# Low parts of some weights by a negative on ScalarE and an accumulating transfer, in place of differences on GpSimd

## The chip, the cores and the metric

The kernel runs on one core of one Trainium2 chip. The metric is the device time of one execution in microseconds (us). The engines are named as the profile names them: PE is TensorE (matmuls; PEld its weight loads), DVE is VectorE, ACT is ScalarE, POOL is GpSimd, SP is SyncE, which here only starts transfers. Each engine works through its own instructions in order.

## The reference

Two layers of an encoder over 512 positions of width 1024, in float32. Cut to what matters here:

```python
mem_n = rms_norm(mem, mem_norm_g)                  # 256 memory tokens
for l in range(2):
    h = rms_norm(x, g_pre_mix[l])
    proj = h @ w_in[l]                             # 1024 x 5632: three attentions' q, k, v, and gates
    ...                                            # neighbourhood (with bias rpb), dilated, memory (mem_n @ w_kv[l])
    x = x + rms_norm(merged @ w_out[l], g_post_mix[l])
    h = rms_norm(x, g_pre_ffn[l])
    u = depthwise_conv_centred(h @ w_up[l], conv_w[l], conv_b[l])
    x = x + rms_norm((gelu(a) * b) @ w_down[l], g_post_ffn[l])
```

## The kernel before

Activations lie transposed in SBUF: channels in the 128 partitions, positions in the free dimension, split into two halves of 256 positions. Every float32 product is made of three products of a shorter format (float32r): each operand is split into a high part (`hi`, rounded) and a low part (`lo`, the value minus `hi`), and `mm3` issues hi·hi, hi·lo and lo·hi into one PSUM bank. So each weight tile of 128x1024 is loaded raw (`wraw`, three buffers, by SP), then cast to `hi` by ScalarE, then `lo` is made by a difference raw - hi, usually on VectorE. This is `split`, called by `weights`. A buffer of `wraw` is free for the next load when its last reader is done.

Most weights are prepared as one tile of 128x1024 (`whi`, `wlo`, two buffers each) while TensorE works on the one before. At two places TensorE would have nothing to do while a norm is computed, and several weight tiles are prepared ahead as two chunks of 128x512 each, into buffers named `m` (or `h`):

- At the start of layer 0: six tiles of `w_in`, those in `FIRST`, called tile one to six below. TensorE multiplies them as three pairs with the first half of the positions as soon as that half is normalised (banks mm, mm, then o, pt, then s, s), then all with the second half. The pair five and six is the group s<-h,m.
- At the handover from layer 0 to layer 1, around the last norm of layer 0: four tiles of `w_kv` (`kv_ahead`) and the same six tiles of `w_in` for layer 1. The tables `KVE` and `GEN` say by letter which engine makes the low part: G for GpSimd, V for VectorE.

The norm needs squares of x (ScalarE), their sum over tiles (`acc`, VectorE), a matmul against a column of 1/1024 (`pt<-mean,acc`, on TensorE in its place in the order), a square root and a reciprocal. At the handover each of the eight tiles of x is first updated (y<-y,pt, then x<-x,y on VectorE).

TensorE's order is fixed by hand (`Woven`: a clock of estimated costs, jobs with due times, explicit order edges). The other engines' order comes from a scheduler that sees the dependences. GpSimd also makes the bias of the neighbourhood attention for each head (`a_bias`: a transfer of `rpb`, then three differences against a mask), copies keys (`ka`, `m`) and adds the gated branches. The bias transfer is held behind GpSimd's last difference of weights, where there is one:

```python
behind(nc.gpsimd.dma_start(out=raw, in_=rpb[l, h]).ins, last_lo.get(G))
```

Lines of the profile that matter: 114 is the line through which every ScalarE and VectorE instruction is issued, 225 a difference of `split`, 230 the raw load, 247 a matmul, 293 and 294 key copies, 455 the memory tokens' transfer (started by ScalarE), 596 and 599 the bias transfer and its differences.

Of the kernel before, what the change touches and what calls it, by code (L numbers as in the profile page):

```python
# [9 lines left out]
AF = mybir.ActivationFunctionType  # L10
ALU = mybir.AluOpType
# [9 lines left out]
KD = D_MODEL // 128  # L21
# [6 lines left out]
FIRST = (0, 3, 4, 7, 6, 1)  # L28
# [6 lines left out]

LAT_QK, LAT_SM, LAT_T, LAT_V, LAT_T2 = 1.0, 4.5, 1.5, 2.0, 0.6
STEP_A, STEP_B, STEP_M = 9.0, 9.0, 5.5
SQG, LOG, GEN, KVE = {0: (), 1: ()}, {0: (), 1: ()}, 'GGVGVG', 'VVGG'
SD1 = 4.0
MARGIN = 0.3  # L40
SB = True
# [1 line left out]
KVD, GWD, NG, LAT1 = 7.3, 1.0, 2, 12.0  # L43
# [76 lines left out]
def tile_hybrid_encoder(ctx, tc, xT, memT, memg, vecs, rpb, w_in, w_kv, w_bra, w_brb, w_brm,  # L120
                        w_out, w_up, w_down, c_ident, c_mask, c_tab0, c_tab1, out):
    nc = tc.nc
# [13 lines left out]
    uid, last_copy, last_act, crit, last_lo = [0], [None], [None], [None], {}  # L136
    wv = Woven(tc)

    def nm(s):
        uid[0] += 1  # L140
        return f"{s}_{uid[0]}"


    def big(dt=F32R, shape=(128, 512)):
        return mp.tile(list(shape), dt, tag="m", name=nm("m"))
# [28 lines left out]
    def f32(ap):  # L174
        return ap.bitcast(F32)

    G = nc.gpsimd
    ACT, V = Counted(nc.scalar, wv, 0.1, 0.8e-3), Counted(nc.vector, wv, 0.065, 1.05e-3)

    DUP, MDUP = G, G  # L180
    MSQ = G

    def ready(least):
# [34 lines left out]
    def behind(ins, other):  # L218

        if other is not None and ins is not other:  # L220
            tc.add_manual_dep(ins, other.name, ORDER, reason="issue order")

    def split(src, hi, lo, eng=None):
        last_copy[0] = ACT.copy(hi, src).ins
        last_lo[eng or V] = (eng or V).tensor_sub(lo, src, f32(hi)).ins

    def weights(src, K, C, slot=None, eng=None, after=None):

        raw = wp.tile([128, K, C], F32, tag="wraw", name=nm("wraw"))
        nc.sync.dma_start(out=raw, in_=src)  # L230
        if slot is None:
            hi = wp.tile([128, K, C], F32R, tag="whi", name=nm("whi"), bufs=2)
            lo = wp.tile([128, K, C], F32R, tag="wlo", name=nm("wlo"), bufs=2)
            split(raw, hi, lo, eng)
            behind(last_copy[0], after)
            return [(hi[:, k, :], lo[:, k, :]) for k in range(K)]
        n = 512 // C
        w = []
        for k in range(0, K, n):
            c = min(n, K - k)  # L240
            hi, lo = slot(F32R, (128, c, C)), slot(F32R, (128, c, C))
            split(raw[:, k:k + c, :], hi, lo, eng)
            w += [(hi[:, i, :], lo[:, i, :]) for i in range(c)]
        return w

# [68 lines left out]
    def sumsq_add(acc, src, first, slot=None, eng=None):  # L314
        if first:
            ACT.activation(acc, src, AF.Square)
        else:
            n = acc.shape[-1]
            sq = slot((128, 256)) if slot else small("sq2", 4) if n == 256 else small("sq", 1, (128, 512))
            ACT.activation(sq, src, AF.Square)  # L320
            (eng or V).tensor_add(acc, acc, sq)
# [34 lines left out]
    def rtile():  # L356
        return tp.tile([128, 512], F32, tag="R", name=nm("R"), bufs=1)
# [6 lines left out]
    def pre_norm_job(l, goff, acc, hs, i):  # L364
        half, box = HALVES[i], []
        yield from rstd_job(acc if isinstance(acc, list) else [acc[:, half]], 256, box)
        for k in range(KD):
            g = g0[:, k:k + 1] if l == 0 and goff == V_PRE else vec[:, l, goff + k:goff + k + 1]
            normed(xh(k, half), g, box[0], hs[k][0][:, half], hs[k][1][:, half],
                   G if k in LOG[l > 0 and goff == V_PRE] else V)  # L370
        crit[0] = last_copy[0]
        yield 1.2
        wv.give(f"h{l}.{goff}.{i}")
# [73 lines left out]
    def h_tiles():  # L447
        return [(htile(), htile()) for _ in range(KD)]


    def mem_norm_job(l, hm, slot):
        raws = []
        for k2 in range(KD // 2):
            t = slot(F32, (128, 2, N_MEM))
            nc.scalar.dma_start(out=t, in_=memT[:, 2 * k2:2 * k2 + 2, :])
            raws += [t[:, 0, :], t[:, 1, :]]
        acc = small("h32", 3)
        for k in range(KD):
            sumsq_add(acc, raws[k], k == 0, None, MSQ if l else V)
        yield 14.0  # L460
        box = []
        yield from rstd_job([acc], N_MEM, box)
        for k in range(KD):
            t = slot(F32R, (128, 2, N_MEM))
            normed(raws[k], mg[:, k:k + 1], box[0], t[:, 0, :], t[:, 1, :])
            hm.append((t[:, 0, :], t[:, 1, :]))
        yield 1.2
        wv.give(f"mem{l}")
# [10 lines left out]
    def mem_kv(l, hm, km, vm, pre=()):  # L479
        wv.need(f"mem{l}")  # L480
        for m in range(4):
            w = pre[m] if pre else weights(w_kv[l, m], KD, 128)
            ps = mmbank((128, N_MEM))
            linear(ps, w, hm, slice(0, N_MEM))
            if m < 2:
                t, u = big(F32R, (128, 2, N_MEM)), big(F32R, (128, 2, N_MEM))
                twice_split(ps, (t[:, 0, :], t[:, 1, :]), (u[:, 0, :], u[:, 1, :]), None, MDUP)
                km.append((t, u))
            else:
                vT = big(F32, (128, 256))  # L490
                ACT.copy(vT, ps)
                wv.spawn(mem_v_job(l, vT, vm))


    def group_weights(srcs, engs):
        return [weights(s, KD, 128, big, e) for s, e in zip(srcs, engs)]
# [19 lines left out]
    def proj(l, m, hs, after=None):  # L516
        w = weights(w_in[l, m], KD, 128, after=after)
        ps = mmbank()
        linear(ps, w, hs)
        return ps  # L520
# [366 lines left out]
    gw = group_weights([w_in[0, m] for m in FIRST[:2]], (V, V))  # L887
# [4 lines left out]
    with tc.issue_after(last_copy[0]):  # L892
        sqs = first_squares(HALVES[1])
    wv.spawn(pre_norm_job(0, V_PRE, sqs, hs, 1), SD1)
    gw += group_weights([w_in[0, m] for m in FIRST[2:]], (V, G, V, G))
    for t, c in ((mask, c_mask), (tab0, c_tab0), (tab1, c_tab1)):
        nc.sync.dma_start(out=t, in_=c)
    hm = []
# [3 lines left out]
    for l in range(depth):  # L902
# [41 lines left out]
        for m in range(KD):  # L944
# [3 lines left out]
            hi, lo = big(), big()  # L948
# [4 lines left out]
        hs, R, gw = h_tiles(), rtile(), []  # L953
# [44 lines left out]
        if l == depth - 1:  # L998
            sublayer_end(l, V_POSTF, w_of, fs, 2, None)
            while wv.jobs:  # L1000
                wv._step()
        else:
            hm, km, vm = [], [], []
            wv.spawn(mem_norm_job(l + 1, hm, htile), 20.0)
            pre, R, raw, box = [], rtile(), [], []

            def then(a, i, l=l, box=box):
                box.extend(h_tiles())
                return pre_norm_job(l + 1, V_PRE, a, box, i)

            gw = []

            def kv_ahead(l=l, pre=pre, gw=gw):
                pre.append(weights(w_kv[l + 1, 0], KD, 128, htile))
                yield KVD
                for i in (1, 2, 3):
                    yield 0.9
                    pre.append(weights(w_kv[l + 1, i], KD, 128, big, G if KVE[i] == 'G' else V))
                wv.give(f"kv{l + 1}")
                for m in range(NG):  # L1020
                    yield GWD
                    gw.extend(group_weights([w_in[l + 1, FIRST[m]]], [G if GEN[m] == 'G' else V]))
                wv.give(f"gw{l + 1}")

            sublayer_end(l, V_POSTF, w_of, fs, 1, [then, (box, raw, R)], (1.4, LAT1), lambda: wv.spawn(kv_ahead()))
            wv.need(f"kv{l + 1}")
            mem_kv(l + 1, hm, km, vm, pre)
            wv.need(f"gw{l + 1}")
            gw += group_weights([w_in[l + 1, m] for m in FIRST[NG:]], [G if e == 'G' else V for e in GEN[NG:]])
            wv.need(f"h{l + 1}.{V_PRE}.0")  # L1030
            hs = box

# [92 lines left out]
```

## Time and profile before

| | |
|---|---|
| median of 3 runs | 1551.14 us (1551.08 to 1551.52) |
| the profiled execution's own time | 1551.73 us |
| its span, first to last instruction | 1550.0 us |
| mean granted clock of TensorE | 0.995 |
| differences of weights on GpSimd | 16, 22.7 us in all |
| bias transfers from GpSimd's queue | 12, of 128 KB |

A row of the timeline gives start, duration (us), engine, line, operation, output<-inputs, shapes and count, and in brackets the idle time before it with what ended it. A row of the waits gives the sum in us, the number of waits and the longest. A row of the stretches gives the stretch, then busy us of PE, PEld, DVE, ACT and POOL (with the instructions that started in it), the granted clock, the share of the 16 DMA engines, and GB/s. A row of a group gives line, engine, operation and count, then busy us, mean ns, and the idle time before it by releaser. A row of a transfer gives its count, size, and the median us from issue to landing.

### The profile page before, as it was taken

Reading aid. Unit: us, or ns where it says so; the run is one execution under the profiler, and the core shown is the slowest. Engines: PE = TensorE matmul, PEld = TensorE weight load, DVE = VectorE, ACT = ScalarE, POOL = GpSimd, SP = SyncE. Lnnn points to the kernel's source line nnn. Section 1 sums busy time; section 2 is a strip of 40 time slices with the busy share of each in tenths; the row PEclk is TensorE's granted clock in tenths of the full one; section 3 lists DMA queues with packets and bytes.
Section 4 is the critical chain, followed back from the end, with each engine's and each line's share of the span. In section 5 each row is a group of like instructions: output and inputs, shape, how many; then the busy total and the mean of one; then the engine's idle time right before and its main releaser. Section 6 shows DMA issues by size and latency. Waiting matters only on the chain.

```text
span 1550.0 us, 20648 instructions
## 1 busy us (share of the span) xinstructions
PE 1522.5 (98%) x7970; PEld 1300.1 (84%) x7970; DVE 951.6 (61%) x1684; ACT 712.7 (46%) x1266; POOL 149.7 (10%) x217
## 2 busy tenths in 40 slices
PE   8999999999999999999989999999999999999997
PEld 7988888888988888888888888888889888888887
DVE  6685676335777777742497756753456977776233
ACT  5565554336544444532355555532354544444231
POOL 3340000110000000000154300002100000000000
PEclk9999999999999999999999999999999999999999
DMA  7221213235113322333431221132350233323331
GB/s 246 89 88 64 62 57 107 84 95 165 53 59 100 100 96 95 118 90 101 129 102 59 78 66 58 61 104 88 102 177 15 82 96 99 101 99 89 99 105 63
DMA packets 45810, 144.91 MB, mean 93 GB/s; under 512 B 5376, under 2 KB 9600, under 8 KB 45712
## 3 DMA queue, kind: packets, MB, share of 16 engines
q1 hardware_dynamic: 43776, 139.85, 28.5%
q10 hardware_dynamic: 1296, 2.10, 0.4%
q0 software_dynamic: 640, 1.64, 0.3%
q8 instruction: 62, 1.02, 0.3%
q14 instruction: 36, 0.29, 0.1%
HBM read 141.48 MB, written 2.10 MB: 93 GB/s over the span
## 4 chain that ended last, share of the span: by engine, by line
PE 91%; DVE 6%; ACT 2%; issue 1%; DMA 0%; SPq 0%; ACTq 0%; DVEq 0%
PE mm L247 80%; PE s L247 4%; PE o L247 3%; PE pt L258 2%; DVE m L114 1%; DVE y L114 1%; PE pt L247 1%; DVE ka L114 1%; DVE x L114 1%; ACT y L114 1%; DVE st L114 0%; DVE acc L114 0%; DMA x<-in_xT_dram 0%; DVE wlo L114 0%; ACT whi L114 0%
## 5 line engine op out<-in xcount | busy, mean ns | idle before, releaser
L247 PE MATMUL mm<-h,whi 128*128 128x512 f32 x2496 | 776.5, 392 | 0.0
L247 PEld LDWEIGHTS mm<-h,whi 128*128 128x128 f32 x2496 | 462.0, 188 | 91.3
L247 PE MATMUL mm<-h,wlo 128*128 128x512 f32 x1248 | 486.9, 390 | 0.0
L114 DVE TENSOR_TENSOR wlo<-wraw,whi 128x1024 fp32r<-128x1024 f32 (+1 forms) x213 | 259.2, 1217 | 284.7 <-ACT whi L114 282.3
L114 ACT CAST whi<-wraw 128x1024 fp32r<-128x1024 f32 (+1 forms) x213 | 221.4, 1040 | 307.8 <-PE mm L247 293.4
L247 PEld LDWEIGHTS mm<-h,wlo 128*128 128x128 f32 x1248 | 234.5, 188 | 49.6
L247 PE MATMUL mm<-m,whi 128*128 128x512 f32 (+1 forms) x800 | 215.1, 356 | 1.0 <-DVE m L114 0.8
L247 PEld LDWEIGHTS mm<-m,whi 128*128 128x128 f32 x800 | 141.8, 189 | 22.8 <-PE mm L247 1.3
L247 PE MATMUL mm<-m,wlo 128*128 128x512 f32 (+1 forms) x400 | 142.1, 355 | 0.0
L114 DVE SCALAR_TENSOR_TENSOR y<-y,vec,y 128x511 f32<-128x511 f32 x176 | 130.5, 748 | 3.5 <-ACT y L114 0.9
L114 DVE TENSOR_TENSOR y<-mm,R 128x512 f32<-128x512 f32 x82 | 56.4, 688 | 68.5 <-PE mm L247 68.5
L247 PEld LDWEIGHTS mm<-m,wlo 128*128 128x128 f32 x400 | 75.5, 189 | 10.9
L802 POOL TENSOR_TENSOR m<-m,y 128x512 f32<-128x512 f32 x28 | 36.1, 1289 | 399.4 <-DVE y L114 399.4
L114 ACT ACTIVATE y<-y,vec 128x512 f32<-128x512 f32 x88 | 71.1, 815 | 2.3 <-DVE y L114 1.9
L247 PE MATMUL mm<-m,m 128*128 128x512 f32 x240 | 63.5, 394 | 0.0
L114 ACT ACTIVATE y<-y 128x512 f32<-128x512 f32 x44 | 27.9, 633 | 71.7 <-DVE y L114 71.3
L114 ACT CAST m<-pt 128x512 fp32r<-128x512 f32 (+1 forms) x72 | 38.6, 541 | 46.8 <-PE pt L258 38.5
L114 ACT ACTIVATE y<-y,st 128x256 f32<-128x256 f32 (+1 forms) x80 | 43.8, 549 | 30.4 <-DVE st L114 28.9
L114 DVE TENSOR_TENSOR acc<-acc,sq 128x256 f32<-128x256 f32 (+1 forms) x80 | 41.1, 514 | 26.6 <-ACT sq L114 24.7
L114 DVE TENSOR_TENSOR m<-pt,m 128x512 fp32r<-128x512 f32 (+1 forms) x72 | 45.1, 630 | 19.9 <-ACT m L114 18.6
L114 ACT CAST m<-y 128x512 fp32r<-128x512 f32 x32 | 19.9, 622 | 72.5 <-DVE y L114 72.5
L247 PE MATMUL mm<-h,m 128*128 128x256 f32 x312 | 49.1, 301 | 2.0 <-ACT h L114 1.0
(154 smaller groups left out, 1789.9 us busy)
## 6 DMA issues: line engine op xcount, KB each, us to landing
wraw<-in_w_in_dram SPq DMA_DIRECT2D x88, 512.0 KB, 3.7
wraw<-in_w_up_dram SPq DMA_DIRECT2D x88, 512.0 KB, 3.6
wraw<-in_w_down_dram SPq DMA_DIRECT2D x32, 512.0 KB, 3.5
wraw<-in_w_out_dram SPq DMA_DIRECT2D x16, 512.0 KB, 3.9
wraw<-in_w_down_dram SPq DMA_DIRECT2D x16, 384.0 KB, 3.1
wraw<-in_w_kv_dram SPq DMA_DIRECT2D x8, 512.0 KB, 4.0
wraw<-in_w_bra_dram SPq DMA_DIRECT2D x16, 192.0 KB, 2.3
x<-in_xT_dram SPq DMA_DIRECT2D x8, 256.0 KB, 7.3
```

The lines of the kernel that those rows point to most:

```text
L114: return op(*args, **kw)
L247: wv.pe(nc.tensor.matmul(ps, a, b, start=first, stop=last), cost)
L258: wv.pe(nc.tensor.transpose(ps[:, 128 * i:128 * i + 128], s, ident), 0.11)
L802: (V if br == 2 and m >= 6 else G).tensor_add(acc[m], acc[m], gs)
```

## The change

A third letter, D, is added. For it ScalarE writes the high part as before, then writes the rounded negative of the raw weight into the buffer of the low part, and a transfer started from GpSimd's queue adds the raw weight from DRAM onto it. So there is no difference on any engine, but the raw weight is read from DRAM a second time (256 KB for a chunk), and the raw buffer's last reader is ScalarE. The tables replace every G: at the start the tiles three to six were V, G, V, G and are V, V, D, D; of `w_kv` the last two were G and are D; of `w_in` for layer 1 the six were G, G, V, G, V, G and are D, D, V, V, D, D.

```diff
-SQG, LOG, GEN, KVE = {0: (), 1: ()}, {0: (), 1: ()}, 'GGVGVG', 'VVGG'
+SQG, LOG, GEN, KVE = {0: (), 1: ()}, {0: (), 1: ()}, 'DDVVDD', 'VVDD'
...
+    ENG = {'G': G, 'V': V, 'D': 'D'}
...
-            split(raw[:, k:k + c, :], hi, lo, eng)
+            if eng == "D":
+                last_copy[0] = ACT.copy(hi, raw[:, k:k + c, :]).ins
+                ACT.activation(lo, raw[:, k:k + c, :], AF.Copy, scale=-1.0)
+                nc.gpsimd.dma_start(out=lo, in_=src[:, k:k + c, :], accum_op=ALU.add)
+            else:
+                split(raw[:, k:k + c, :], hi, lo, eng)
...
-    gw += group_weights([w_in[0, m] for m in FIRST[2:]], (V, G, V, G))
+    gw += group_weights([w_in[0, m] for m in FIRST[2:]], (V, V, 'D', 'D'))
...
-                    pre.append(weights(w_kv[l + 1, i], KD, 128, big, G if KVE[i] == 'G' else V))
+                    pre.append(weights(w_kv[l + 1, i], KD, 128, big, ENG[KVE[i]]))
...
-                    gw.extend(group_weights([w_in[l + 1, FIRST[m]]], [G if GEN[m] == 'G' else V]))
+                    gw.extend(group_weights([w_in[l + 1, FIRST[m]]], [ENG[GEN[m]]]))
...
-            gw += group_weights([w_in[l + 1, m] for m in FIRST[NG:]], [G if e == 'G' else V for e in GEN[NG:]])
+            gw += group_weights([w_in[l + 1, m] for m in FIRST[NG:]], [ENG[e] for e in GEN[NG:]])
```

The change moves instructions on GpSimd, ScalarE and VectorE; TensorE's and SP's orders stay. Numbers behind names tell tiles apart. First GpSimd's queue at the start, before: four differences (tiles four and six, two chunks each), then for two heads the bias transfer and its differences.

```order
L225 TENSOR_TENSOR m_62_255<-wraw_60_252,m_61_254 128x512
L225 TENSOR_TENSOR m_64_259<-wraw_60_252,m_63_258 128x512
L225 TENSOR_TENSOR m_72_275<-wraw_70_272,m_71_274 128x512
L225 TENSOR_TENSOR m_74_279<-wraw_70_272,m_73_278 128x512
L596 DMA y_164_925<-in_rpb_dram 128x256
L599 TENSOR_TENSOR y_163_924<-mask_106,y_164_925 128x256 x2
L599 TENSOR_TENSOR y_164_925<-mask_106,y_164_925 128x256
L596 DMA y_180_1008<-in_rpb_dram 128x256
```

The same place with the change; m_67 and m_69 are the low parts of tile five, m_72 and m_74 those of tile six.

```order
L602 DMA y_164_929<-in_rpb_dram 128x256
L605 TENSOR_TENSOR y_163_928<-mask_106,y_164_929 128x256 x2
L605 TENSOR_TENSOR y_164_929<-mask_106,y_164_929 128x256
L602 DMA y_180_1012<-in_rpb_dram 128x256
L246 DMA m_67_265<-in_w_in_dram 128x512
L246 DMA m_69_270<-in_w_in_dram 128x512
L605 TENSOR_TENSOR y_179_1011<-mask_106,y_180_1012 128x256 x2
L605 TENSOR_TENSOR y_180_1012<-mask_106,y_180_1012 128x256
L246 DMA m_72_277<-in_w_in_dram 128x512
L246 DMA m_74_282<-in_w_in_dram 128x512
```

Both bias transfers have moved ahead of the weights' low parts, and the low parts of tile six stand behind six bias differences, the last three of which wait for the second bias transfer.

Second, ScalarE at the handover, before: casts of the third and fourth w_kv tile and of the first w_in tile among the squares of x (acc and sq2).

```order
L114 CAST m_1335_6926<-wraw_1332_6920 128x512
L114 CAST m_1345_6981<-wraw_1344_6979 128x512
L114 CAST m_1347_6985<-wraw_1344_6979 128x512
L114 ACTIVATE acc_1202_6081<-x_85 128x256
L114 ACTIVATE sq2_1337_6940<-x_85 128x256
L114 CAST m_1350_7003<-wraw_1349_7001 128x512
L114 ACTIVATE sq2_1338_6945<-x_85 128x256
L114 CAST m_1352_7007<-wraw_1349_7001 128x512
```

With the change, the same tiles; each ACTIVATE of m from wraw is a negative.

```order
L114 ACTIVATE m_1334_6927<-wraw_1332_6924 128x512
L114 CAST m_1335_6931<-wraw_1332_6924 128x512
L114 ACTIVATE m_1336_6932<-wraw_1332_6924 128x512
L114 CAST m_1345_6987<-wraw_1344_6985 128x512
L114 ACTIVATE m_1346_6988<-wraw_1344_6985 128x512
L114 ACTIVATE acc_1202_6085<-x_85 128x256
L114 ACTIVATE sq2_1337_6946<-x_85 128x256
L114 CAST m_1347_6992<-wraw_1344_6985 128x512
L114 ACTIVATE sq2_1338_6951<-x_85 128x256
L114 ACTIVATE m_1348_6993<-wraw_1344_6985 128x512
```

A negative follows each cast, so the squares of x stand further back in ScalarE's queue.

Third, GpSimd at the end of the handover, before: the differences of the sixth w_in tile, then layer 1's first bias.

```order
L225 TENSOR_TENSOR m_1415_7265<-wraw_1413_7262,m_1414_7264 128x512
L225 TENSOR_TENSOR m_1417_7269<-wraw_1413_7262,m_1416_7268 128x512
L596 DMA y_1472_7760<-in_rpb_dram 128x256
L599 TENSOR_TENSOR y_1471_7759<-mask_106,y_1472_7760 128x256 x2
L599 TENSOR_TENSOR y_1472_7760<-mask_106,y_1472_7760 128x256
```

With the change; m_1410 and m_1412 belong to the fifth w_in tile, m_1415 and m_1417 to the sixth.

```order
L602 DMA y_1472_7776<-in_rpb_dram 128x256
L246 DMA m_1410_7267<-in_w_in_dram 128x512
L246 DMA m_1412_7272<-in_w_in_dram 128x512
L605 TENSOR_TENSOR y_1471_7775<-mask_106,y_1472_7776 128x256 x2
L246 DMA m_1415_7279<-in_w_in_dram 128x512
L605 TENSOR_TENSOR y_1472_7776<-mask_106,y_1472_7776 128x256
L246 DMA m_1417_7284<-in_w_in_dram 128x512
```

The bias transfer is now ahead, and the sixth tile's low parts stand behind bias differences that wait for it.

## The prediction

> **What bounds the kernel now.** I read the page first (busy shares), then the waits of TensorE by stretch, then the timeline around the two places where the changed weights are prepared, and last the granted clock there.
>
> ```profile
> span 1550.0 us, 20648 instructions
> PE 1522.5 (98%) x7970; PEld 1300.1 (84%) x7970; DVE 951.6 (61%) x1684; ACT 712.7 (46%) x1266; POOL 149.7 (10%) x217
> PE pt L247 <- DVE acc L114: 4.6, 2, 3.5
> ```
>
> TensorE is busy 98% of the span, so a change off TensorE can only give or take its waits. Between 750 and 840 us, where layer 0 hands over to layer 1, the last row names the largest: 4.6 us in two waits for VectorE's sum of squares. Between 24 and 60 us, the start's second part, the list of TensorE's waits is empty: anything that comes late there is new loss. These two stretches hold all sixteen differences that the change takes from GpSimd.
>
> The handover in the timeline:
>
> ```profile
> 768.30 6.93 POOL L225 TENSOR_TENSOR m<-wraw,m 128x512 fp32r<-128x512 f32 x5 [105.56 <-ACT m L114]
> 776.61 4.24 POOL L225 TENSOR_TENSOR m<-wraw,m 128x512 fp32r<-128x512 f32 x3 [1.39 <-ACT m L114]
> ...
> 770.41 2.22 DVE L114 TENSOR_TENSOR x<-x,y 128x256 f32<-128x256 f32 x2
> 772.56 0.74 DVE L114 TENSOR_TENSOR y<-y,pt 128x256 f32<-128x256 f32 x2
> 776.43 0.41 DVE L114 TENSOR_TENSOR x<-x,y 128x256 f32<-128x256 f32 x1
> 776.88 1.40 DVE L114 TENSOR_TENSOR acc<-acc,sq 128x256 f32<-128x256 f32 x1
> 779.65 1.83 DVE L114 TENSOR_TENSOR x<-x,y 128x256 f32<-128x256 f32 x2
> ...
> 777.09 3.04 PE L247 MATMUL mm<-h,m 128*128 128x256 f32 x24
> 783.59 0.58 PE L247 MATMUL pt<-mean,acc 128*128 128x1 f32 x4 [3.46 <-DVE acc L114]
> 813.64 0.58 PE L247 MATMUL pt<-mean,acc 128*128 128x1 f32 x4 [1.16 <-DVE acc L114]
> ```
>
> The same VectorE addition takes 0.41 us at 776.43, when GpSimd waits, and about 1.1 each (2.22 for two) while GpSimd subtracts; y<-y,pt, whose second input lies in PSUM, keeps its pace (0.74 for two). So GpSimd's differences stretch VectorE's additions with two SBUF inputs, and TensorE, done at 777.09 + 3.04 = 780.13, waits until 783.59. The wait has a second price:
>
> ```profile
> 785.00:788.60 3.60, 3.50 (x19) 3.21 (x18) 3.17 (x10) 1.44 (x5) 2.13 (x6) 0.55 0.02 5
> 872.00:877.00 5.00, 3.88 (x14) 3.20 (x15) 2.95 (x4) 2.12 (x3) 2.97 (x6) 0.66 0.00 0
> 873.12 0.55 PE L258 MATMUL pt<-ident,y 128*128 128x128 f32 x3 [2.09 <-DVE y L114]
> ```
>
> The third number from the end is the granted clock: 0.55 in 785.0 to 788.6, behind the wait of 3.46, so 3.6 x 0.45 = 1.6 us are lost (1.7 below, with the dip's edges). Behind the wait of 2.09 at 873 it was 0.66 in 872 to 877, 5 x 0.34 = 1.7. Behind the wait of 1.16 nothing comparable stands. Waits of 2 us and more cost about 1.7 more.
>
> **The change at the handover.** Six tiles of 128x1024 (two of w_kv, four of w_in) lose their GpSimd differences; ScalarE writes twelve negatives, and GpSimd's queue starts twelve transfers.
>
> ```profile
> L225 POOL TENSOR_TENSOR m<-wraw,m 128x512 fp32r<-128x512 f32 x16 | 22.7, 1445 | 128.8 <-ACT m L114 120.5 <-PE s L258 8.4
> 768.51 1.65 ACT L114 CAST m<-wraw 128x512 fp32r<-128x512 f32 x3
> L114 ACT CAST m<-wraw 128x512 fp32r<-128x512 f32 x18 | 10.4, 615 | 0.0
> L114 ACT ACTIVATE sq<-x 128x256 f32<-128x256 f32 x14 | 5.7, 416 | 8.3 <-DVE x L114 6.7 <-DVE acc L114 1.7
> ```
>
> GpSimd gives up 16 x 1.445 us in all for 16 issues (0.61 each by the rpb rows below). VectorE's additions return to 0.41. What decides instead is ScalarE: from 768.51 to the eighth square of x it now has 7 negatives and 6 casts among the 8 squares. A negative of the same shape is not in the trace; by the cast's 0.55 (1.65 for three, back to back) to 0.615 (mean) that is 13 x 0.55 + 8 x 0.375 = 10.2 to 13 x 0.615 + 8 x 0.416 = 11.3 us, so the last square ends at 778.7 to 779.8, and VectorE's last addition 0.41 later, at 779.1 to 780.2. TensorE arrives at 780.13. The wait of 3.46 falls to 0 or 0.1, and with it the 1.7 of clock. The margin is under 1 us; ScalarE is late next. The 1.16 at 813.64, behind additions stretched likewise, goes too. Sum: -3.5 - 1.7 - 1.2 = -6.4 us.
>
> Against that stands the last of the six tiles. In GpSimd's queue its two transfers now stand behind a transfer of the bias and two bias differences of layer 1.
>
> ```profile
> 794.71 0.69 DVE L114 TENSOR_TENSOR m<-wraw,m 128x512 fp32r<-128x512 f32 x1
> 797.38 1.51 DVE L114 TENSOR_TENSOR x<-x,y 128x256 f32<-128x256 f32 x1
> 808.18 2.62 POOL L599 TENSOR_TENSOR y<-mask,y 128x256 f32<-128x256 f32 x3 [3.79 <-DVE ka L114]
> 804.44 5.92 PE L247 MATMUL s<-h,m 128*128 128x256 f32 x48
> wraw<-in_w_in_dram SPq DMA_DIRECT2D x88, 512.0 KB, 3.7
> y<-in_rpb_dram POOLq DMA_DIRECT2D x3, 128.0 KB, 2.3
> ```
>
> All before it moves up by 3.5 + 1.7 = 5.2. Its raw tile is loaded once VectorE's difference at 794.71 has freed a buffer: 795.40 - 5.2 + 3.7 = 793.9; cast and negative end at 795.1. The bias transfer waits for the addition at 797.38, without stretch 797.38 + 0.41 - 5.2 = 792.6, and lands 2.3 to 2.9 later (2.3 was the median around the handover); two bias differences of 2.62/3 bring 796.7 to 797.2. Then the transfer of the low part. An accumulating one is not in the trace: 256 KB lie between 128 KB at 2.9 and 512 KB at 3.7, so 3.3, and 7.0 at worst (the row in the next part). It lands at 800.0 to 804.2. TensorE's group starts at 804.44 - 5.2 = 799.2 and its sixth matmul, 5 x 0.123 later, reads that low part: a stall of 0.2 to 4.3. I take 2.0, above the low end, because three raw loads, released earlier by ScalarE than they were by GpSimd, share the rings. Behind it on GpSimd TensorE needs nothing soon: the first copies of ka come at 824.14.
>
> ```profile
> 824.14 0.62 POOL L293 CAST ka<-ka 64x512 fp32r<-64x512 f32 x1 [8.68 <-ACT ka L114]
> 46.33 0.69 POOL L293 CAST ka<-ka 64x512 fp32r<-64x512 f32 x1
> DMA packets 45810, 144.91 MB, mean 93 GB/s; under 512 B 5376, under 2 KB 9600, under 8 KB 45712
> ```
>
> The other two rows serve the next part.
>
> **The change at the start.** Tiles three and four go to VectorE, which gives tile five away: no cost seen, the first four's matmuls have their operands. Tile five and six get their low parts by transfer, and the queue order is new: the bias transfers used to stand behind the differences, and now stand ahead.
>
> ```profile
> 21.28 2.54 DVE L114 TENSOR_TENSOR y<-y,y 128x256 f32<-128x256 f32 x6
> 24.45 0.33 SPq L230 DMA_DIRECT2D wraw<-in_w_in_dram  x1
> 28.90 2.91 POOL L225 TENSOR_TENSOR m<-wraw,m 128x512 fp32r<-128x512 f32 x2 [2.08 <-ACT m L114]
> 31.23 5.92 PE L247 MATMUL s<-h,m 128*128 128x256 f32 x48
> 31.76 0.61 POOL L596 DMA_DIRECT2D y<-in_rpb_dram  x1
> 33.25 0.33 ACTq L455 DMA_DIRECT2D m<-in_memT_dram  x1
> 38.85 2.32 POOL L599 TENSOR_TENSOR y<-mask,y 128x256 f32<-128x256 f32 x3 [6.48 <-DVE h L114]
> 31.00:38.80 7.80, 7.80 (x68) 7.80 (x67) 5.34 (x13) 3.39 (x9) 1.37 (x2) 1.00 0.75 253
> DMA to landing us min/median/max: 2.8/2.9/7.0
> ```
>
> The last row is that of the bias transfers up to 66 us. Step by step: the first bias transfer waits for the first of six additions, 21.28 + 0.42 = 21.7, lands at 24.6; three differences of 2.32 end at 26.9; the second transfer starts and lands at 29.8; behind it two transfers for tile five, then three differences that wait for that landing, until 32.1; only then tile six's first low part is started. (Its negative is earlier: raw tile at 24.45 + 3.7 = 28.2, casts and negatives after it.) It lands 3.3 to 7.0 later, at 35.4 to 39.1. TensorE's sixth matmul wants it at 31.23 + 5 x 0.123 = 31.85. The stall is 3.6 to 7.3. I take 5.5, the middle: the transfer of 7.0 is the one issued at 31.76, when the rings were 0.75 busy, and memT's transfers, whose last was issued at 33.25, now start later and meet it. Behind so long a wait the clock dips: +1.7. What else waits on GpSimd (ka's copies, from 46.33) is not reached. Nothing later waits by the clock on the wall, so the 7.2 are not given back.
>
> The skill gives another price for that transfer. The Trainium skill, "DMA: Bandwidth & Descriptors", section "Anatomy of one DMA — SWDGE (gpsimd) path", fits 2.0 us + bytes/436e3; for 256 KB that is an estimate of 2.6, a stall of 2.9 and a sum lower by 2.6. The 2.3 around the handover would agree with it, the 7.0 does not.
>
> The 16 transfers read 16 x 0.26 = 4.2 MB again, against 144.91 MB moved: no bound.
>
> **Sum.** Start +5.5 + 1.7, handover -6.4 + 2.0 = +2.8 us. The profiled execution took 1551.73 (1.73 around its span), 0.6 above the median of the runs, 1551.14; there the sum gives 1554.0.
>
> For the 2.0 at the handover no dip is counted, though the row at 873 had one behind 2.09; with it the sum is +4.5, 1555.6. The Trainium skill, "TensorE: Matmul & The Clock Gate", section "Part 1: The HAM clock gate", wants a whole idle window of some 3.4 us before the clock halves; by that neither 2.0 nor 2.09 would cost a dip, and here the trace differs.
>
> **The rivals.**
> - Quiet rings, the other side: every software transfer lands in 2.3. Then at the start 24.0, 26.3, 28.6, 30.9, and the low part at 30.9 + 2.6 (2.3 and the 0.3 that twice the bytes may cost) = 33.5: a stall of 1.6, short enough for no dip, and 0.2 at the handover: 1.6 - 6.4 + 0.2 = -4.6, 1546.5. It decides once the transfer lands before 34. For it speaks 2.3 at the handover, against it the 0.75 share of the rings. The Trainium skill's fit above points this way.
> - Busy rings: 7.0 for the transfers that matter: 7.3 + 1.7 - 6.4 + 4.3 + 1.7 = +8.6, 1559.7. For it speaks the one row that fell into this traffic; a read, an addition and a write per element may be slower than a copy.
> - ScalarE takes VectorE's place: its in-order queue holds squares behind casts that wait for a raw tile. If the second w_in tile, whose load starts three ScalarE instructions after 768.51, at 770.2, and whose cast comes after 11 casts or negatives and 6 squares, at 768.51 + 11 x 0.55 + 6 x 0.375 = 776.8, is later than that, every us of that goes into the wait; with 3.5 us of it the 5.2 return, +8.0, 1559.1. Against it: 6.6 us of room for a load of 3.7.
>
> **How the numbers follow.** A change within 0.2% (3.1 us) is about what a measurement of this kernel cannot tell from none: 1548.0 to 1554.2. The forecast (start stall 3.6 to 7.3, handover wait gone: 1551 to 1557) has 0.55, of it 0.33 within the bound and 0.22 above; quiet rings 0.13 (0.10 faster, 0.03 same); busy rings 0.18 (0.16 slower, 0.02 same); ScalarE late 0.14 (0.11 slower, 0.03 same). Together faster 0.10, same 0.41, slower 0.49. The range runs from half of the quiet case, 1548.5, to 1560.5, just above the busy one. The likeliest's own range is 1551 to 1557.
>
> **What would show it.** In the trace after: near 31.8 us a TensorE wait of 3.6 to 7.3 on a transfer into m, and a clock near 0.5 after it; no wait at the statistics near 780 (plus the shift) and VectorE's x<-x,y at 0.41; a wait of 0.2 to 4.3 in the group before the raw half. The prediction is wrong if the start shows no wait, if the wait for acc remains, or if a transfer lands far outside 2.3 to 7.0.

## The result, and the profile after

The changed kernel took 1565.0 us (median of 4 runs) against 1551.33: a ratio of 1.0085, with a 95% interval of 1.0067 to 1.0102. It is slower by 13.7 us, outside the predicted range. The two profiled executions differ by a little more, 1564.7 against 1550.0, so 14.7 in their spans. The line numbers of the code are 6 higher than before (a matmul is L253, a raw load L231, the bias transfer L602, its differences L605), and the accumulating transfer is L246. Here are the span, TensorE's share, and the transfers that GpSimd starts (count, size, median us to landing), from the page; the last row is that of all sixteen accumulating ones.

```profile
span 1564.7 us, 20682 instructions
PE 1525.0 (97%) x7970; PEld 1302.1 (83%) x7970; DVE 943.2 (60%) x1684; ACT 718.1 (46%) x1282; POOL 141.0 (9%) x217
m<-in_w_in_dram POOLq DMA_DIRECT2D x12, 256.0 KB, 8.4
m<-in_w_kv_dram POOLq DMA_DIRECT2D x4, 256.0 KB, 8.3
DMA to landing us min/median/max: 5.0/8.3/11.1
```

TensorE's waits of the changed kernel; the first row is the start (24 to 60 us, where there was none before), the other two are the whole list of the handover (740 to 850 us, where 4.6 us on acc stood):

```profile
PE s L253 <- DMA m<-in_w_in_dram: 10.0, 2, 6.6
PE s L253 <- DMA m<-in_w_in_dram: 5.3, 2, 4.3
PE mm L253 <- DMA m<-in_w_in_dram: 1.2, 1, 1.2
```

Two rows of the kernel before, the first matmuls behind the start's group s<-h,m and the first matmul of a mean at the handover:

```profile
36.99 5.20 PE L247 MATMUL mm<-h,m 128*128 128x256 f32 x42
767.81 0.50 PE L247 MATMUL pt<-mean,acc 128*128 128x1 f32 x4
```

The timeline of the changed kernel at both places (TensorE, GpSimd, and VectorE's last sum), which answers to these and to the rows at 31.23, 783.59 and 804.44 of before:

```profile
26.77 0.57 POOL L602 DMA_DIRECT2D y<-in_rpb_dram  x1
27.34 1.85 POOL L246 DMA_DIRECT2D m<-in_w_in_dram  x2
32.56 2.09 POOL L605 TENSOR_TENSOR y<-mask,y 128x256 f32<-128x256 f32 x3 [3.37 <-DMA y<-in_rpb_dram]
34.60 1.75 POOL L246 DMA_DIRECT2D m<-in_w_in_dram  x2
34.06 0.62 PE L253 MATMUL s<-h,m 128*128 128x256 f32 x3 [3.33 <-DMA m<-in_w_in_dram]
41.30 7.36 PE L253 MATMUL s<-h,m 128*128 128x256 f32 x43 [6.62 <-DMA m<-in_w_in_dram]
48.49 5.20 PE L253 MATMUL mm<-h,m 128*128 128x256 f32 x42
...
779.55 0.50 PE L253 MATMUL pt<-mean,acc 128*128 128x1 f32 x4
790.36 0.43 DVE L114 TENSOR_TENSOR acc<-acc,sq 128x256 f32<-128x256 f32 x1 [0.40 <-ACT sq L114]
791.72 0.50 PE L253 MATMUL pt<-mean,acc 128*128 128x1 f32 x4
...
805.57 0.57 POOL L602 DMA_DIRECT2D y<-in_rpb_dram  x1 [9.65 <-DVE x L114]
806.13 1.80 POOL L246 DMA_DIRECT2D m<-in_w_in_dram  x2
813.38 0.87 POOL L246 DMA_DIRECT2D m<-in_w_in_dram  x1
818.44 7.84 PE L253 MATMUL s<-h,m 128*128 128x256 f32 x43 [4.28 <-DMA m<-in_w_in_dram]
```

The granted clock (third number from the end) and the rings' share (the last but one) in four stretches:

```profile
36.00:41.00 5.00, 0.00 (x0) 0.00 (x0) 1.68 (x4) 1.95 (x6) 0.35 (x1) 0.50 1.04 286
41.00:45.50 4.50, 4.20 (x19) 4.20 (x20) 3.66 (x6) 2.61 (x4) 0.00 (x0) 0.50 0.13 18
792.00:796.00 4.00, 4.00 (x35) 4.00 (x36) 3.75 (x11) 2.72 (x9) 3.70 (x9) 1.00 1.08 284
816.00:823.50 7.50, 5.06 (x23) 5.06 (x24) 2.06 (x6) 0.56 (x2) 3.56 (x12) 0.58 0.39 72
```

The share of the rings (the 16 DMA engines) is the recorded time of the packets. Above 1 the records overlap, so that part of a packet's time may then be waiting.

The reader is to see three things. First, where the time went. The matmul of the mean that stood at 767.81 before stands at 779.55: 11.7 us were lost up to there, and 11.5 of them already at the matmuls behind the start's group (48.49 against 36.99). Of these, 10.0 are waits and about 2.1 the clock at 0.50 from 41.3 to 45.5 at least, less 0.9 by which the group began earlier; 0.3 is left over. Of the other 3.0 us the handover has 2.7 (the first matmuls behind it are at 843.73 against 829.26, 14.5 later): 6.5 of waits and about 2.5 of slow clock (43 matmuls of 0.12 us take 7.7 from 818.44 on, up to 826.12), less the 4.6 + 1.7 that are gone. Second, the first wait for acc is gone as forecast: the last sum ends at 790.79, and the mean at 791.72 waits for nothing. Third, each wait ends with a transfer into m that was issued 5 to 10 us before, while the rings are about full: 27.34 to 34.0, 34.60 to 41.3, 806.13 to 813.5 and 813.38 to 818.4, and at the wait of 1.2 the first low part of the second w_in tile, 790.32 to 800.3. The bias transfers in front of the low parts are late too: the one issued at 26.77 landed 5.7 us later, the one at 805.57 5.5 later.

### The profile page after: what moved, and what is told of

It reads as the page before. It is cut to its first block, busy times and chain, and to the rows that moved or that the text cites. A ratio compares the mean times of both kernels' runs of the same rounds, so it can differ in the third digit from the quotient of the medians.

```text
span 1564.7 us, 20682 instructions
## 1 busy us (share of the span) xinstructions
PE 1525.0 (97%) x7970; PEld 1302.1 (83%) x7970; DVE 943.2 (60%) x1684; ACT 718.1 (46%) x1282; POOL 141.0 (9%) x217
## 4 chain that ended last, share of the span: by engine, by line
PE 89%; DVE 5%; DMA 3%; ACT 2%; issue 1%; POOL 0%; SPq 0%; ACTq 0%; POOLq 0%
PE mm L253 78%; PE s L253 5%; PE o L253 3%; PE pt L264 2%; DVE m L114 2%; DMA m<-in_w_in_dram 1%; DVE y L114 1%; PE pt L253 1%; DVE ka L114 1%; ACT y L114 1%; DVE st L114 1%; DMA x<-in_xT_dram 0%; DVE wlo L114 0%; DMA wraw<-in_w_in_dram 0%; ACT whi L114 0%
## 5 line engine op out<-in xcount | busy, mean ns | idle before, releaser
L253 PE MATMUL mm<-h,whi 128*128 128x512 f32 x2496 | 776.6, 392 | 0.0
L253 PEld LDWEIGHTS mm<-h,whi 128*128 128x128 f32 x2496 | 461.8, 188 | 90.9
L253 PE MATMUL mm<-h,wlo 128*128 128x512 f32 x1248 | 486.9, 390 | 0.0
L253 PEld LDWEIGHTS mm<-h,wlo 128*128 128x128 f32 x1248 | 234.5, 188 | 49.8
L253 PE MATMUL mm<-m,whi 128*128 128x512 f32 (+1 forms) x800 | 215.1, 356 | 0.9 <-DVE m L114 0.8
L253 PEld LDWEIGHTS mm<-m,whi 128*128 128x128 f32 x800 | 141.8, 189 | 22.8 <-PE mm L253 1.3
L253 PE MATMUL mm<-m,wlo 128*128 128x512 f32 (+1 forms) x400 | 142.1, 355 | 0.0
L253 PEld LDWEIGHTS mm<-m,wlo 128*128 128x128 f32 x400 | 75.5, 189 | 10.8
L253 PE MATMUL s<-h,m 128*128 128x256 f32 x336 | 52.0, 304 | 15.2 <-DMA m<-in_w_in_dram 15.2
L253 PE MATMUL mm<-m,m 128*128 128x512 f32 x240 | 63.5, 394 | 0.0
L253 PEld LDWEIGHTS s<-h,m 128*128 128x128 f32 x336 | 47.3, 210 | 16.1 <-DMA m<-in_w_in_dram 16.1
L114 ACT ACTIVATE y<-y,st 128x256 f32<-128x256 f32 (+1 forms) x80 | 43.6, 546 | 31.4 <-DVE st L114 31.3
```

The costliest lines, as they stand in the source:

```text
L114: return op(*args, **kw)
L253: wv.pe(nc.tensor.matmul(ps, a, b, start=first, stop=last), cost)
```

## The experiments

The two theories after the result were these. A: an accumulating transfer is itself dear, in the rings' time and in the time to its landing. B: the crowd is dear, that is, 256 KB more per tile beside raw loads, or GpSimd's queue with the bias transfers ahead.

**The start alone, and the handover alone.** In the first the tables of the handover are those of before, in the second the start is.

```diff
-SQG, LOG, GEN, KVE = ..., 'DDVVDD', 'VVDD'
+SQG, LOG, GEN, KVE = ..., 'GGVGVG', 'VVGG'      # the first
-    ... (V, V, 'D', 'D'))
+    ... (V, G, V, G))                            # the second
```

> The transfers at the start of layer 0 only; the handover as before. Theory (the loss is made where the accumulating transfers land late): the start's two waits of 3.3 and 6.6 us stay, with a clock near 0.5 behind them, and all later work comes 11.7 us later, as in the changed kernel at its handover; the handover's wait of 3.5 for acc is back. 1551.3 + 11.7 = 1563.0. Rival (the two places cost each other something, over buffers or GpSimd's queue): the time differs by more than 2 us from that.

Measured: 1563.22, ratio 1.0078 (1.0062 to 1.0093), as expected, and the waits for acc are back at 4.6. The start's waits are 8.3 and not 10.0, since the group began 1.7 later in this execution (32.00 against 30.33); it ends as in the changed kernel, with the matmuls behind it at 48.38.

> The transfers at the handover only; the start as before. Theory: 14.7 - 11.7 = 3.0 us are lost here, since waits of 5.3 and 1.2 on the low parts and a slow clock behind them outweigh the waits for acc that go: 1554.3, with landings near 8. Rival (the handover was only upset by the late start, my prediction's 2.3 to 3.3 us landings hold without it): waits on low parts under 1 us, 1546 to 1548.

Measured: 1552.32, ratio 1.0009 (0.9998 to 1.0021): the time lies between the two expectations, and cannot be told from the kernel before. The waits decide between the theories. This is TensorE's list from 740 to 850 us, and the landing of its twelve transfers:

```profile
PE s L253 <- DMA m<-in_w_in_dram: 4.4, 2, 3.7
PE pt L264 <- ACT sq L114: 0.9, 1, 0.9
PE mm L253 <- DMA m<-in_w_in_dram: 0.7, 1, 0.7
PE mm L253 <- ACT y L114: 0.5, 1, 0.5
...
DMA to landing us min/median/max: 4.1/8.9/10.5
```

The late low parts are no echo of the late start; together with the slow clock behind them (0.54 in 808 to 812) they take back what the handover gains. The two ratios add up to that of the whole change (0.78% + 0.09% against 0.85%).

**Plain copies in place of accumulating ones.**

```diff
-                nc.gpsimd.dma_start(out=lo, in_=src[:, k:k + c, :], accum_op=ALU.add)
+                nc.gpsimd.dma_start(out=lo, in_=src[:, k:k + c, :])
```

> The changed kernel with the transfers as plain copies of the same bytes onto the same tiles, with no accumulation: the low part holds the raw value, so part of the product is left wrong, the order of work is the same. Theory A (the accumulation itself is dear: the rings move it at about half the rate): landings fall from 8.3 to about 3 to 5 and the rings' share falls below 1 in the crowded stretches; time 1549 to 1556. Theory B (the crowd is dear: 256 KB more per tile beside raw loads of 512 KB, or GpSimd's queue): landings stay at 7 to 8, time 1562 to 1566.

The low part then holds the raw weight, so the product is wrong and only the time counts. Measured: 1558.15, ratio 1.0046 (1.0030 to 1.0063): between the two, so each has about half. Tile six's first low part landed 3.8 us after its issue at the start and 3.7 at the handover, where the accumulating one took 6.6 and 5.0. The bias transfers in front of it stayed late, 5.6 and 5.9. Landing of the sixteen, and the software queue's bytes and share of the span, of this kernel and then of the changed one:

```profile
DMA to landing us min/median/max: 3.2/5.8/7.4
q0 software_dynamic: 2944, 5.84, 1.3%
```

```profile
q0 software_dynamic: 2944, 5.84, 2.0%
```

The queue takes 0.013 x 1555.2 = 20.2 us of all 16 rings here and 0.020 x 1564.7 = 31.3 in the changed kernel, for the same bytes in the same packets. With VectorE alone at the handover (below), where the queue carries only the bias, it takes 0.004 x 1545.9 = 6.2. So a plain copy costs (20.2 - 6.2)/16 = 0.9 us of all rings and an accumulating one (31.3 - 6.2)/16 = 1.6; the shares are rounded to 0.1%, which leaves 0.1 on each, and some of it may be waiting; the next run is free of that.

**The same transfer where nothing is crowded.** In the kernel before, one transfer per two tiles of the up projection, onto a tile that nothing reads:

```diff
...
+                    ACT.activation(probe[0], raw[:, 0:4, :], AF.Copy, scale=-1.0)
+                    if pcount[0] % 4 == 0:
+                        nc.gpsimd.dma_start(out=probe[0], in_=src[:, 0:4, :], accum_op=ALU.add)
+                    else:
+                        nc.gpsimd.dma_start(out=probe[0], in_=src[:, 0:4, :])
```

> The kernel before with 26 extra transfers of 256 KB on GpSimd's queue during the up projection of both layers, one per two weight tiles, alternately accumulating and plain, each behind a negative on ScalarE; nothing reads them. TensorE should not wait: 1551 to 1553. Theory A: accumulating ones land about 2 us or more later than plain ones, even with the rings 0.3 busy (5 or more against about 3). Theory B: both land alike, near 3, and only the crowd made them 8.

Measured: 1549.9 (one run). The first two rows are the 13 plain ones, the next two the 13 accumulating ones (GpSimd's time for the issue, then landing). The last two are the stretches of one plain and one accumulating transfer, issued at 402.54 and 416.63:

```profile
L244 POOL DMA_DIRECT2D ka<-in_w_up_dram x13: 543/543/562, 402.5 to 1313.4; - x13
DMA to landing us min/median/max: 2.7/3.4/3.9
```

```profile
L242 POOL DMA_DIRECT2D ka<-in_w_up_dram x13: 863/873/917, 416.6 to 1324.3; - x13
DMA to landing us min/median/max: 3.7/5.8/6.1
```

```profile
402.00:410.00 8.00, 8.00 (x71) 8.00 (x70) 7.95 (x24) 5.95 (x17) 0.55 (x1) 1.00 0.11 33
416.00:424.00 8.00, 8.00 (x69) 8.00 (x68) 7.63 (x23) 5.47 (x16) 0.91 (x1) 1.00 0.21 33
```

Theory A is shown: 5.8 against 3.4 to landing, and 0.87 against 0.54 for the issue. In either stretch the transfer is all that moves (33 GB/s in 8 us are 264 KB), and it takes 8 x 0.11 = 0.9 us of all rings plain and 8 x 0.21 = 1.7 accumulating: the price is the transfer's own and not the crowd's. The crowd then adds as much again to the median landing: 3.4 becomes 5.8 and 5.8 becomes 8.3.

**The bias transfers behind, as they stood before.**

```diff
-                nc.gpsimd.dma_start(out=lo, ..., accum_op=ALU.add)
+                last_lo['D'] = nc.gpsimd.dma_start(out=lo, ..., accum_op=ALU.add).ins
-        behind(nc.gpsimd.dma_start(out=raw, in_=rpb[l, h]).ins, last_lo.get(G))
+        behind(nc.gpsimd.dma_start(out=raw, in_=rpb[l, h]).ins, last_lo.get('D', last_lo.get(G)))
```

> The changed kernel with the bias transfers held behind the accumulating ones in GpSimd's queue, as they stood behind its differences before. Theory (two causes: the transfer's own 8 us and the queue order): tile six's transfers start when ScalarE's negative is done, near 29 instead of 34.6 at the start and near 808 instead of 813.4 at the handover, and still land 6.5 to 8 later; the start's waits fall from 10.0 to about 5, the handover's from 6.5 to about 1.5, half-rate clock stays at the start: 1565.0 - 5.2 - 5.2 = 1554.6. Rival (the rings are the only bound, so an earlier start only queues longer): landings grow to 11 or more, time 1561 to 1565.

Measured: 1561.09, ratio 1.0070 (1.0054 to 1.0085), which is the rival's time and, by its interval, not clear of the changed kernel's. The issue of tile six's first low part and the wait for it, at the start and at the handover:

```profile
27.65 0.86 POOL L246 DMA_DIRECT2D m<-in_w_in_dram  x1 [1.15 <-ACT m L114]
37.16 6.95 PE L253 MATMUL s<-h,m 128*128 128x256 f32 x43 [4.96 <-DMA m<-in_w_in_dram]
802.86 0.86 POOL L246 DMA_DIRECT2D m<-in_w_in_dram  x1 [0.58 <-ACT m L114]
811.49 6.92 PE L253 MATMUL s<-h,m 128*128 128x256 f32 x43 [3.36 <-DMA m<-in_w_in_dram]
...
DMA to landing us min/median/max: 6.8/9.2/10.5
```

At the start the waits fell from 10.0 to 5.6, as expected: issued 7.0 earlier, the low part landed 4.1 earlier. At the handover they fell only from 6.5 to 4.3 and not to 1.5, and this low part took 8.6 in place of 5.0. Issued earlier, the transfers queue longer: the median landing grew from 8.3 to 9.2. The same edit at the handover alone:

> Transfers at the handover only, bias behind them. Theory: of the 4.4 us in the group s<-h,m about 3.5 go, with the 2 us of slow clock behind them: 1552.3 - 5.5 = 1546.8, faster than before by 0.3%. Rival (rings): waits on low parts stay at 4, time 1551 to 1553.

Measured: 1551.22, ratio 1.0005 (0.9994 to 1.0015). The rival is right: a single wait of 5.2 us stands in the group s<-h,m, and the landings go to 11.5. My theory that the queue order is worth 5 us there fell.

**Both at once:** plain copies and the bias behind them.

> The changed kernel with both mended at once: plain copies in place of the accumulating transfers, so that the low part holds the raw value and part of the product is left wrong, and the bias transfers behind them. If the two causes only add: 1565.0 - 6.9 - 3.9 = 1554.2. Theory (one bound, the rings' time: a plain copy takes 0.9 us of all 16 rings, an accumulating one 1.6): with less queued ahead the earlier start counts in full, landings near 5 and waits on low parts of 0 to 2 at either place, 1548 to 1552. Rival (the crowd of raw loads alone): landings stay near 6, waits of 3 to 5 at the start, 1555 to 1558.

Measured: 1553.37, ratio 1.0017 (1.0008 to 1.0027), with waits of 3.2 at the start and 2.3 at the handover. Again the low part holds the raw weight. The causes add within the noise, and the theory of one bound, which wanted waits of 0 to 2, does not hold in this form. The four ratios side by side:

| | bias ahead | bias behind |
|---|---|---|
| accumulating | 1.0085 | 1.0070 |
| plain copy | 1.0046 | 1.0017 |

So of some 13 us the accumulation makes 6 to 8, the order 2 to 5, and 2.6 remain for a second, plain trip of the weights. Each ratio is known to about 0.15%, 2.3 us, so the order's lower figure is not clear of noise. The 2.6 are the median's; the profiled execution of this kernel was a short one (1551.2, its span 0.7 below that of the kernel before) without a clock dip behind its waits, so where they lie was not seen. Its ten runs go from 1550.14 at a mean clock of 0.997 to 1555.67 at 0.990, so it may be the clock; this is not shown.

**VectorE in GpSimd's place.** Start as before (V, G, V, G); at the handover no low part by GpSimd.

```diff
-SQG, LOG, GEN, KVE = ..., 'DDVVDD', 'VVDD'
+SQG, LOG, GEN, KVE = ..., 'DDVVVV', 'VVDD'      # transfers for four tiles, bias behind
+SQG, LOG, GEN, KVE = ..., 'VVVVVV', 'VVVV'      # no transfer
```

> The start as before; at the handover the transfers for two w_kv and the first two w_in tiles, VectorE's differences for the other four w_in tiles, none on GpSimd. Theory: neither the waits for acc nor those on transfers in s<-h,m are there; VectorE has 4 x 0.68 = 2.7 us more near 800, which it has free: 1546 to 1547. Rival (VectorE late for the second half's norm): a wait of 1 to 3 near 815, 1548 to 1551.

Measured: 1547.74, ratio 0.9982 (0.9974 to 0.9991). The rival's wait is there, 1.5 us for acc at the second norm, with a clock dip behind it.

> The start as before; at the handover no transfers and no GpSimd: all low parts by VectorE. Theory (GpSimd's differences stretched VectorE's additions, and that made the wait for acc): VectorE has 8 x 0.68 = 5.4 us more up to 785 but about 8 additions less stretched by 0.7 each, 5.6 us: the wait of 3.5 falls to 0 to 2 and the clock dip with it; 1546 to 1549. Rival (VectorE was the bound by its own load): the wait grows to 5 or more, 1553 and above.

Measured: 1546.99, ratio 0.9976 (0.9967 to 0.9984). TensorE's mean and VectorE around the first norm of the handover, and the wait at the second:

```profile
776.49 0.68 DVE L114 TENSOR_TENSOR m<-wraw,m 128x512 fp32r<-128x512 f32 x1
777.09 0.41 DVE L114 TENSOR_TENSOR acc<-acc,sq 128x256 f32<-128x256 f32 x1
779.68 0.51 PE L253 MATMUL pt<-mean,acc 128*128 128x1 f32 x4
809.86 0.58 PE L253 MATMUL pt<-mean,acc 128*128 128x1 f32 x4 [1.87 <-DVE acc L114]
```

With 5.4 us more of its own VectorE is in time for the first norm, since acc<-acc,sq takes 0.41 and not 1.40. That GpSimd's subtractions caused the wait of 3.46 is shown: without them it is gone, though VectorE has more to do. The remedy needs no transfer.

**VectorE everywhere, and three mixtures of it.**

```diff
-    ... (V, V, 'D', 'D'))
+    ... (V, V, V, V))   with 'VVVVVV', 'VVVV'   # the first
+    ... (V, G, V, G))   with 'VVVGVG', 'VVVV'   # the second
+    ... (V, G, V, G))   with 'VVVVVV', 'VVDD'   # the third
```

> No transfer and no GpSimd difference anywhere: VectorE makes all low parts, at the start too. Theory: at the start no engine is late either way, the bias stands ahead and costs nothing: as with VectorE alone at the handover, 1546 to 1548. Rival (VectorE late at the start by 4 x 0.68): waits of 1 to 3 near 30, 1548 to 1551.

Measured: 1547.02, ratio 0.9969 (0.9959 to 0.9979). No wait at the start.

> The start as before; at the handover VectorE alone for the part ahead of the first norm (w_kv, the first two w_in tiles), GpSimd for tiles four and six of the part behind it, as before. Theory: the wait of 3.5 stays gone, the wait of 1.9 with its clock dip that VectorE alone has at the second norm becomes the 1.2 without dip of before: 1545 to 1546.5. Rival (GpSimd's differences stretch VectorE's additions there by as much as they save): 1547 to 1549.

Measured: 1549.10, ratio 0.9988 (0.9980 to 0.9997). The rival is right, and more than that: the wait for acc at the second norm is 3.1, not 1.2, and longer than the 1.9 without GpSimd.

> The start as before; at the handover transfers for the two w_kv tiles only (four transfers in place of twelve), VectorE for all w_in tiles. Theory (the landing time comes from the rings' queue): with half the transfers of that part in flight they land in 6 to 7 instead of 8.2, 10 us ahead of their use, and cost nothing: time as with VectorE alone, 1546 to 1548. Rival (8 us belongs to the transfer in this place): landings stay at 8, time the same.

Measured: 1544.53, ratio 0.9960 (0.9948 to 0.9972), the fastest here and faster than both kernels. Its transfers, their landing, TensorE's longest wait of the handover, and the rings in the stretch:

```profile
L246 POOL DMA_DIRECT2D m<-in_w_kv_dram x4: 866/879/935, 769.7 to 773.7; - x4
DMA to landing us min/median/max: 7.3/8.3/9.1
PE pt L253 <- DVE acc L114: 1.3, 1, 1.3
776.00:780.00 4.00, 4.00 (x36) 4.00 (x35) 4.00 (x11) 3.27 (x8) 0.05 (x1) 1.00 1.10 269
```

Its time is the theory's or better, its landings are the rival's: with four transfers in place of eight in that part they still land in 8.3, and the rings are at 1.10 while they run. But TensorE waits for none of the low parts of w_kv, and VectorE is spared four differences of 0.68, 2.7 us. The intervals overlap with those of VectorE alone at the handover (0.9976) and everywhere (0.9969), so whether the four transfers themselves bring anything is not settled. One difference in the profiles is that the wait of 1.3 has no clock dip behind it, and the 1.9 with VectorE alone has.

## Why the prediction was wrong

- **The landing of the transfers in GpSimd's queue: the step that failed.** The prediction let the bias transfers land in 2.9 us (start) and 2.3 to 2.9 (handover), and the low part behind them in 3.3 to 7.0, taken as about 5.2. The bias transfers took 5.7 and 5.5. The low parts of tile six took 6.6 and 5.0, inside the range, but others, which got no delay at all, took up to 11.1. The rows behind the low figures were copies in quieter microseconds. "256 KB lie between 128 KB at 2.9 and 512 KB at 3.7, so 3.3" also took plain transfers for an accumulating one, which takes 5.8 alone. I wrote in a rival that a read, an addition and a write may be slower than a copy, and gave that no number.
- **"4.2 MB again, against 144.91 MB moved: no bound"** put the crowd at nothing: it set the bytes against the whole span. At the start the rings went from 0.75 (31 to 38.8 us, before) to 1.04 (36 to 41, after), and an accumulating byte takes 1.6/0.9 of the time of a copied one. Whether the bias transfers were held up by the low parts behind them or by the raw loads beside them, no run tells apart: they were as late beside plain copies (5.6 and 5.9).
- **The start.** The mechanism held: tile six's transfer behind the bias, TensorE waiting in s<-h,m, a slow clock after it. Its term was 5.5 + 1.7 and measured 10.0 + 2.1. The second bias transfer was issued when I said (26.77, by the working 26.9), but for its late landing tile six's first low part was started at 34.60 and not at 32.1, 2.5 late; its own landing of 6.6 is 1.4 above the one taken; and TensorE came 0.9 earlier. Together that is 4.8 on top of 5.5, against 10.0 of idle time (0.4 of the stall counts as busy matmuls). Tile five, to which I gave no delay, was late by 3.3, but this only splits the stall in two: TensorE would have waited for tile six all the same.
- **The handover's gain.** -3.5 - 1.7 came as worked out: VectorE's additions at the first norm back at 0.41, no wait for acc, no dip. The -1.2 of the second norm shows less: there TensorE came late itself. It would have been there near 820.2 without the waits and the slow clock of s<-h,m (an estimate: 812.13, where that group starts, and the 8.0 from there to the end of the matmuls before the mean in the kernel before), and the last sum was done at 818.35.
- **The handover's loss.** Taken as 2.0 without a dip, measured 6.5 with 2.5 of slow clock. 1.2 of it is the second w_in tile, whose low part landed 9.9 after its issue and to which I gave no delay. The bias transfer did wait for the addition as I said (issued at 805.57, which is 792.6 and the 11.7 of the start and the 1.2 of that wait), but it landed 5.5 us later and not 2.3, so that tile six's low part was started 3 to 4 us late. From there it took the 5.0 that I had taken for it.
- **The clock.** "Waits of 2 us and more cost about 1.7 more" rested on two rows and is no rule: see the last section.
- **The rivals.** Busy rings (1559.7, 0.18) was the nearest one, and 5 short: its 7.0 was right for tile six at the start, but it too left the bias transfers at 2.9 and 2.3. Quiet rings fell; the fit of the Trainium skill, "DMA: Bandwidth & Descriptors", section "Anatomy of one DMA — SWDGE (gpsimd) path", behind it gives an estimate of 2.6 for 256 KB, where the plain transfer alone took 3.4. ScalarE late did not come: the last sum was done 0.9 us before TensorE arrived, a margin as thin as I said. Of the bounds, half of the quiet case's gain would be 1548.8 and not 1548.5; nothing hangs on it.

## What to carry to other kernels

When a change moves work to an operation that the trace does not hold, measure it alone first; a row of a cheaper relative is a lower bound. Weigh new transfers against the share of the rings in the microseconds in which they run, not against the span; let the transfers that already stand in the queue land later too, and put new ones where their result is wanted ten microseconds later. Before moving work off an engine that slows another, try the simplest taker: VectorE alone beat both kernels, by 0.2 to 0.3% against the kernel before.

## What the runs showed of the hardware

- An accumulating transfer of 256 KB took 1.6 to 1.7 us of all rings against 0.9 for a copy, 0.87 us of GpSimd's queue against 0.54, and landed 2.4 us later when alone (5.8 against 3.4).
- VectorE's additions of 128x256 with both inputs in SBUF took up to 1.5 us beside GpSimd's subtractions and 0.41 without them.
- The clock's dip does not follow the length of the wait. In the kernel with four tiles by transfer it fell to 0.62 and 0.53 behind a wait of 1.45; in the one with plain copies and the bias behind it it stayed at 1.00 behind one of 2.48, in the group s<-h,m that had a dip in the changed kernel:

```profile
809.16 0.58 PE L253 MATMUL pt<-mean,acc 128*128 128x1 f32 x4 [1.45 <-DVE acc L114]
810.00:812.00 2.00, 2.00 (x14) 2.00 (x12) 0.17 (x1) 0.04 (x1) 0.00 (x0) 0.62 0.00 0
812.00:814.00 2.00, 2.00 (x12) 2.00 (x11) 1.31 (x4) 1.16 (x4) 0.00 (x0) 0.53 0.00 0
```

```profile
34.26 3.12 PE L253 MATMUL s<-h,m 128*128 128x256 f32 x24 [2.48 <-DMA m<-in_w_in_dram]
34.00:36.00 2.00, 1.74 (x14) 1.74 (x15) 0.00 (x0) 0.24 (x1) 0.00 (x0) 1.00 1.09 382
```

The Trainium skill, "TensorE: Matmul & The Clock Gate", section "Part 1: The HAM clock gate", asks for an idle window of some 3.4 us; the dip behind 1.45 does not agree with that. What decides is left open. Such dips may be one reason why the runs of one kernel differ by some microseconds; this was not tested.
